# A two-layer encoder trunk on one core: moving the tiles in SBUF, weights to 0 and tokens to 64 modulo 128 bytes

## The chip, the cores and the metric

One core of a Trainium2 chip runs the whole program. The metric is the device time of one execution in microseconds; the kernel before takes 1598.72 us, the median of 3 runs (1597.99 to 1599.84).

## What is computed

Two encoder layers over 256 frames of width 1024, in float32. Layer 0 mixes with gated linear attention and retention and has a dense SwiGLU of width 3584; layer 1 mixes with a gated DeltaNet and has a mixture of 8 SwiGLU experts of width 3584, two for each frame.

```python
def swiglu(x, w_gu, w_down):
    gt, up = jnp.split(x @ w_gu, 2, axis=-1)
    return (jax.nn.silu(gt) * up) @ w_down

def reference(x, positions, ...):
    # layer 0
    h = mixer_gla_retention(x, positions, ab_w_in[0], ..., ab_w_out[0])
    x = layer_norm(DEEPNORM_ALPHA * x + h, ab_ln1_g[0], ab_ln1_b[0])
    x = layer_norm(DEEPNORM_ALPHA * x + swiglu(x, ffn_w_gu[0], ffn_w_down[0]), ...)
    # layer 1
    h = mixer_gated_deltanet(x, c_w_in[0], c_conv_w[0], ..., c_w_out[0])
    x = layer_norm(DEEPNORM_ALPHA * x + h, c_ln1_g[0], c_ln1_b[0])
    y = moe_swiglu(x, moe_w_router[0], moe_b_router[0], moe_w_gu[0], moe_w_down[0])
    return layer_norm(DEEPNORM_ALPHA * x + y, c_ln2_g[0], c_ln2_b[0])
```

## The kernel before

The work is a chain of large products with weights that are read once: mixer 0, the dense FFN, mixer 1, and the expert layer, which has most of the weights. To keep float32 accuracy every weight and every token value is split into a high and a low part of type `float32r`, and a product is three matmuls: high by high, low by high, high by low (`mm3`, `mm3w`).

Weights come in pieces of 1 MiB, one DMA each, into the tiles `wraw` (`load`). A piece is cut into two halves of 1024 columns for each partition (`cut`): ScalarE copies a half into `wh` (the high part), VectorE subtracts and writes `wl` (the low part). The halves go in turn through a ring of five buffers (`set_ring`): three lie in the pool `spl`, on the left of SBUF, two in the pool `keep`, on the right. In the expert layer the ring has only the three of `spl`, since `keep` is closed there (end of `mixer1`). A half is loaded again only when its matmuls are done.

Which operand moves through TensorE and which is stationary differs by stage:

- mixers 0 and 1, input and output projections (`proj`, `out_proj`): the weights move, up to 512 columns a matmul; the tokens are stationary (`xh`, `xl` in `keep`, in mixer 0's output projection `oh`, `ol`);
- dense FFN, gate and up (`ffn`, `gu`), and mixer 1's q, k and v: the tokens `xh`, `xl` move, 256 columns a matmul, and the weights are stationary; a half gives 24 matmuls;
- dense FFN, down: the weights move, 512 columns; the tokens `hh`, `hl` are stationary;
- expert layer (`gate_up_mm`, `down_mm`): the weights move, 512 columns; the tokens `xgh`, `xgl` and `hh`, `hl` (of the pool `mb`) are stationary.

The order of instructions on every engine is written out by the program itself (`manual_schedule`), with a planner (`Pace`) that counts on costs for each operation. Where a tile lies is not planned: pools are stacked one behind the other, from the left or from the right end, and a tile lies where the sum of the tiles before it puts it. In the operand names of the profile the moving operand stands first: `psA<-wh,xgh` moves `wh` past `xgh`.

Of the kernel before, what the change touches and what calls it, by code (L numbers as in the profile page):

```python
# [9 lines left out]
F32 = mybir.dt.float32  # L10
# [7 lines left out]
P = 128  # L18
# [97 lines left out]
FI = 6, 3, 3  # L116
GA = 1
FILL = 5, 1
class Pace:


# [2 lines left out]
    def __init__(self, nc):  # L124
        self.nc = nc
        self.clk = dict(tensor=0.0, vector=0.0, scalar=0.0, gpsimd=0.0, sync=0.0)
        self.spans, self.rings, self.base = {}, {}, {}
        self.cold, self.ops = 3000.0, 0
        for e in self.clk:
            setattr(self, e, Paced(self, e))  # L130
# [111 lines left out]
class Net:  # L242
    NSPL, NDENSE = 5, 2

    def __init__(self, ctx, tc, a, out):
        self.ctx, self.tc, self.nc, self.a, self.out = ctx, tc, Pace(tc.nc), a, out
        pool = lambda **k: ctx.enter_context(tc.tile_pool(**k))
        self.const = pool(name="const", bufs=1)
        self.slots = []
        self.raw_pool("raw", 3)  # L250
        self.spl = pool(name="spl", bufs=1)
        self.xe = pool(name="xe", bufs=2)
        self.ln = pool(name="ln", bufs=2)

        self.dense = ExitStack()
        self.keep = self.dense.enter_context(tc.tile_pool(name="keep", bufs=1, side="right"))
        self.ring = []
        self.psum = pool(name="psum", bufs=4, space=bass.MemoryType.PSUM)
        self.cst = {}
        self.tasks, self.live, self.tagB = [], 0, None  # L260
        self.pieces, self.halves, self.ready, self.loaded = [], [], {}, {}
        self.share, self.lows, self.pend = False, [], None
        self.n_dma = self.n_split = self.n_use = self.held = 0
# [180 lines left out]
        return t  # L444

    def bc(self):
        return self.keep.tile([P, D], F32, name="bc", tag="bc", bufs=2)

    def rstd(self, y, var, eps=EPS):
# [236 lines left out]
    def load_x(self):  # L686
        nc, a = self.nc, self.a
        self.load_const("cb", self.const, nc.sync)
        self.x = [self.new_x(0, b) for b in range(2)]
        for b in range(2):  # L690
            for c in range(2):
                cs = slice(c * 512, (c + 1) * 512)
                nc.sync.dma_start(self.x[b][:, cs], a["x"][b * P:(b + 1) * P, cs])
            if b == 0:
                self.load_next(1)
        self.xh = self.keep.tile([P, KT, T], F32R, name="xh", tag="xh")
        self.xl = self.keep.tile([P, KT, T], F32R, name="xl")
        self.load_next()

    def transpose_x(self, b, between=lambda: None):  # L700
# [6 lines left out]
    def mixer0(self):  # L707
# [4 lines left out]
        pool = es.enter_context(self.tc.tile_pool(name="m0", side="right", bufs=1))  # L712
        tmp = es.enter_context(self.tc.tile_pool(name="m0t", side="right", bufs=2))
        oh = pool.tile([P, KT, T], F32R, name="oh")
        ol = pool.tile([P, KT, T], F32R, name="ol")
        wg2 = pool.tile([17, 256], F32, name="wg2")
        nc.sync.dma_start(wg2[0:16], a["gla_w_gate2"])
        nc.sync.dma_start(wg2[16:17], a["gla_b_gate"].rearrange("(o n) -> o n", o=1))
# [276 lines left out]
        n_ = {k: c1 - c0 for k, (c0, c1) in self.AB.items()}  # L995
        self.fill(att[0][0][:, 0:P], FILL[0])
        self.held = 3
        engs = [nc.vector, nc.gpsimd]
        self.transpose_x(0, lambda: (self.fill(att[0][0][:, 0:P], FILL[1]), self.presplit(1, engs.pop(0))))
        pt = [self.ps("A") for _ in range(2)]  # L1000
# [640 lines left out]
    def moe_open(self):  # L1641

        nc, a, tc = self.nc, self.a, self.tc
        self.raw_pool("raw2", RO)
        self.load_next()
        self.mo = mo = self.ctx.enter_context(tc.tile_pool(name="mo", bufs=1))
        self.wr = mo.tile([P, KT, NE], F32, name="wr")
        nc.gpsimd.dma_start(self.wr, a["moe_w_router"].rearrange("(k p) e -> p k e", p=P))
        self.br = mo.tile([P, NE], F32, name="br")
        nc.gpsimd.dma_start(self.br, a["moe_b_router"].partition_broadcast(P))  # L1650
        self.load_const("c2", mo, nc.gpsimd)
        self.tri, self.one = self.c("tri0"), self.c("one").to_broadcast([P, P])
        self.xnh = [mo.tile([P, D], F32R, name="xnh", tag="xnh", bufs=2) for _ in range(2)]
        self.xnl = [mo.tile([P, D], F32R, name="xnl", tag="xnl", bufs=2) for _ in range(2)]
        self.lg = mo.tile([P, 2, NE], F32, name="lg")
        self.sel = mo.tile([P, 2, NE], F32, name="sel")
        self.comb = mo.tile([P, 2, NE], F32, name="comb")
        self.slot = mo.tile([P, 2, NE], F32, name="slot")
        self.t1 = mo.tile([P, 2], F32, name="t1")
        self.mx = mo.tile([P, 1], F32, name="mx")  # L1660
        self.cnt = mo.tile([P, 2, NE], F32, name="cnt")

    def natural_parts(self, b, x):

        self.nc.scalar.activation(self.xnh[b], x, AF.Copy)
        self.nc.gpsimd.tensor_tensor(self.xnl[b], x, self.xnh[b].bitcast(F32), OP.subtract)
# [390 lines left out]
    def moe_rest(self):  # L2057

        nc, a, tc = self.nc, self.a, self.tc
        slots, n = self.slots, [0]  # L2060

        def pieces(srcs):
            for src in srcs:
                wv = self.load(slots[n[0] % len(slots)], src)
                n[0] += 1
                for i in range(2):
                    yield self.cut(wv, i, 2)

        def run(gen):
            for _ in gen:  # L2070
                self.nc.clk["tensor"] += 50.0

        most = nc.values_load(self.most[0:1, 0:1], min_val=0, max_val=T)
        with tc.If(most > P):
            with tc.For_i(0, NE, 1) as e:
                pick = self.mb.tile([P, NE], F32, name="pick")
                nc.sync.dma_start(pick, a["eye"][bass.ds(e, 1)].rearrange("o n -> (o n)").partition_broadcast(P))
                t2 = self.mb.tile([P, 2, NE], F32, name="t2")
                sc = self.mb.tile([P, 2, 2], F32, name="sc")
                pb = pick[:, None, :].to_broadcast([P, 2, NE])  # L2080
                for i, src in enumerate((self.slot, self.comb)):
                    nc.vector.tensor_tensor(t2, src, pb, OP.mult)
                    nc.vector.tensor_reduce(sc[:, i], t2, axis=mybir.AxisListType.X, op=OP.add)
                nc.vector.tensor_scalar(sc[:, 0], sc[:, 0], -float(P), None, OP.add)
                s = self.new_s()[:, :, 0:P]
                self.onehot(s, 0, lambda b: sc[:, 0, b:b + 1])
                xg = self.new_xg()
                run(self.gather(s, [xg], [0]))
                acc = [self.ps("B") for _ in range(2)]
                wg = a["moe_w_gu"][bass.ds(e, 1)].rearrange("o k n -> (o k) n")  # L2090
                wd = a["moe_w_down"][bass.ds(e, 1)].rearrange("o k n -> (o k) n")
                for c in CUT:
                    pts = []
                    for u in range(2):
                        pt = [self.ps("A") for _ in range(c[1] // 512)]
                        for j, w in enumerate(pieces(self.gate_up(wg, c, u))):
                            self.gate_up_mm(pt, c, xg, j, w)
                            self.flush()
                        pts.append(pt)
                    hs = []  # L2100
                    run(self.hidden(self.silu(pts[0]), pts[1], hs))
                    for j, w in enumerate(pieces(self.down_rows(wd, c))):
                        self.down_mm(acc, c, hs, j, w)
                        self.flush()
                        self.hfree += j % 4 == 3
                st = []
                run(self.flip(s, st))
                run(self.scatter(st, acc, lambda b: sc[:, 1, b:b + 1]))
            for b in range(2):
                for c in range(2):  # L2110
                    self.ln_stats(self.y[b], self.st[:, b], c)
# [88 lines left out]
```

## Time and profile before

| | |
|---|---|
| time, median of 3 runs | 1598.72 us (1597.99 to 1599.84) |
| the profiled execution | 1597.8 us, of which the span from the first to the last instruction is 1596.0 |
| TensorE matmul | busy 1555.4 us, 97% of the span, 8467 instructions |
| TensorE weight load | 1332.8 us, 84% |
| VectorE | 1301.3 us, 82% |
| ScalarE | 1050.6 us, 66% |
| GpSimd | 160.5 us, 10% |
| DMA | 444.81 MB, mean 279 GB/s |
| mean granted TensorE clock | 0.992 |

Busy time is a share of the whole span, over stages with different limits, so the stages are read one by one. A busy TensorE says little by itself: the ends of matmuls are modelled and consecutive matmuls overlap in the trace, so what a matmul costs is read from the distance between two starts.

### The profile page before, as it was taken

What the parts mean: (1) busy time and instruction counts of PE and PEld (TensorE: products, weight loads), DVE (VectorE), ACT (ScalarE), POOL (GpSimd) and SP (SyncE); (2) the same over time, 40 slices, a digit from 0 to 9 for tenths busy, and PEclk for the clock granted to TensorE, in tenths of its full rate; (3) what the DMA queues carried; (4) which work ended last, traced back from release to release, by engine and by line L of the source; (5) the groups of instructions that cost most, each with busy time, mean ns of one, the idle gap of its engine ahead of it and who ended that gap; (6) DMA issues with size and microseconds to landing.
All of it is one profiled execution on the core that took longest, in us unless ns stands there. A gap on an engine that the chain in (4) does not pass through costs nothing.

```text
span 1596.0 us, 22720 instructions
## 1 busy us (share of the span) xinstructions
PE 1555.4 (97%) x8467; PEld 1332.8 (84%) x8467; DVE 1301.3 (82%) x1541; ACT 1050.6 (66%) x1239; POOL 160.5 (10%) x231
## 2 busy tenths in 40 slices
PE   9999999998999989999999999999999999999995
PEld 7788999997999968888888888888888888888884
DVE  5667555558867877999989999989999998999997
ACT  5345444445643347877877877878877778777774
POOL 5233000002361540000000000000000000000001
PEclk9999999999999989999999999999999999999998
DMA  7446555556313678999999999999999999999960
GB/s 265 134 159 223 190 198 192 185 168 198 97 47 106 226 275 294 376 370 350 372 347 341 367 368 362 367 362 335 369 368 363 360 375 328 369 366 368 361 219 28
DMA packets 161992, 444.81 MB, mean 279 GB/s; under 512 B 7553, under 2 KB 53778, under 8 KB 161874
## 3 DMA queue, kind: packets, MB, share of 16 engines
q1 hardware_dynamic: 160338, 437.98, 76.0%
q0 software_dynamic: 1536, 5.31, 1.1%
q8 instruction: 68, 1.11, 0.3%
q14 instruction: 50, 0.41, 0.1%
HBM read 442.21 MB, written 1.05 MB: 278 GB/s over the span
## 4 chain that ended last, share of the span: by engine, by line
PE 59%; issue 3%; DMA 0%; POOL 0%; DVE 0%; POOLq 0%; DVEq 0%
PE psA L223 37%; PE psB L223 21%; DMA gb<-in_c_ln_g_dram 0%; POOL x L223 0%; DVE wl L223 0%; POOLq L2196 0%; DVE xgl L223 0%; POOLq L223 0%; DVEq L223 0%
## 5 line engine op out<-in xcount | busy, mean ns | idle before, releaser
L223 DVE SCALAR_TENSOR_TENSOR wl<-wraw,wh 128x1024 fp32r<-128x1024 f32 (+2 forms) x824 | 992.7, 1223 | 199.0 <-ACT wh L223 147.1
L223 ACT ACTIVATE wh<-wraw 128x1024 fp32r<-128x1024 f32 (+3 forms) x835 | 863.1, 1052 | 265.2 <-PE psA L223 201.3
L223 PE MATMUL psA<-wh,xgh 128*128 128x512 f32 x894 | 291.0, 395 | 0.0
L223 PE MATMUL psA<-wh,xgl 128*128 128x512 f32 x894 | 288.3, 392 | 0.0
L223 PE MATMUL psA<-wl,xgh 128*128 128x512 f32 x894 | 279.4, 394 | 0.0
L223 PEld LDWEIGHTS psA<-wh,xgl 128*128 128x128 f32 x894 | 168.2, 188 | 37.2
L223 PEld LDWEIGHTS psA<-wh,xgh 128*128 128x128 f32 x894 | 166.9, 189 | 34.5
L223 PEld LDWEIGHTS psA<-wl,xgh 128*128 128x128 f32 x894 | 165.9, 188 | 34.8
L223 PE MATMUL psB<-wh,hh 128*128 128x512 f32 x560 | 183.3, 392 | 0.0
L223 PE MATMUL psB<-wh,hl 128*128 128x512 f32 x560 | 183.0, 392 | 0.0
L223 PE MATMUL psB<-wl,hh 128*128 128x512 f32 x560 | 182.8, 392 | 0.0
L223 PE MATMUL psA<-xh,wh 128*128 128x256 f32 x608 | 172.8, 284 | 0.0
L223 PE MATMUL psA<-xh,wl 128*128 128x256 f32 x608 | 170.0, 280 | 0.0
L223 PE MATMUL psA<-xl,wh 128*128 128x256 f32 x608 | 169.9, 280 | 0.0
L223 PEld LDWEIGHTS psB<-wh,hl 128*128 128x128 f32 x560 | 105.0, 188 | 23.5 <-DVE hl L223 0.9
L223 PEld LDWEIGHTS psB<-wl,hh 128*128 128x128 f32 x560 | 104.5, 188 | 22.3
L223 PEld LDWEIGHTS psB<-wh,hh 128*128 128x128 f32 x560 | 103.8, 188 | 20.6
L223 PEld LDWEIGHTS psA<-xh,wh 128*128 128x128 f32 x608 | 115.0, 189 | 1.4 <-issue 0.5
L223 PEld LDWEIGHTS psA<-xl,wh 128*128 128x128 f32 x608 | 115.0, 189 | 0.5
L223 PEld LDWEIGHTS psA<-xh,wl 128*128 128x128 f32 x608 | 115.0, 189 | 0.0
L223 POOL TENSOR_TENSOR x<-x,gb 128x256 f32<-128x256 f32 x4 | 4.2, 1069 | 993.8 <-ACT x L223 993.6
L223 PE MATMUL psA<-wh,xh 128*128 128x512 f32 (+4 forms) x224 | 74.1, 359 | 2.2 <-ACT wh L223 1.7
(298 smaller groups left out, 1449.5 us busy)
## 6 DMA issues: line engine op xcount, KB each, us to landing
wraw<-in_moe_w_gu_dram SPq DMA_DIRECT2D x224, 1024.0 KB, 6.2
wraw<-in_moe_w_down_dram SPq DMA_DIRECT2D x110, 1024.0 KB, 6.0
wraw<-in_ffn_w_gu_dram SPq DMA_DIRECT2D x26, 1024.0 KB, 5.1
wraw<-in_ffn_w_down_dram SPq DMA_DIRECT2D x14, 1024.0 KB, 4.9
wraw<-in_c_w_in_dram SPq DMA_DIRECT2D x12, 1024.0 KB, 5.7
wraw<-in_ab_w_in_dram SPq DMA_DIRECT2D x10, 1024.0 KB, 5.3
wraw<-in_ab_w_out_dram SPq DMA_DIRECT2D x4, 1024.0 KB, 4.9
wraw<-in_c_w_out_dram SPq DMA_DIRECT2D x4, 1024.0 KB, 7.0
```

What stands on the lines that cost most here:

```text
L223: r = f(*args, **kw)
```

## The change

Six tiles that nothing reads or writes are put into pools, and so the tiles that are allocated behind them move. No instruction is added or removed, and the rows of every engine's instruction stream, with their waits, are the same one by one.

```diff
+GAP = 16, 56, 8, 16
 ...
         self.const = pool(name="const", bufs=1)
+        self.const.tile([P, 24], F32, name="gap2")
 ...
-        self.ring = []
+        self.ring, self.gap = [], None
 ...
     def bc(self):
+        if not self.gap:
+            self.gap = self.keep.tile([P, GAP[1]], F32, name="gap1")
         return self.keep.tile([P, D], F32, name="bc", tag="bc", bufs=2)
 ...
         self.xl = self.keep.tile([P, KT, T], F32R, name="xl")
+
+        self.keep.tile([P, GAP[0]], F32, name="gap0")
 ...
         ol = pool.tile([P, KT, T], F32R, name="ol")
+        pool.tile([P, GAP[2]], F32, name="gap3")
 ...
         self.cnt = mo.tile([P, 2, NE], F32, name="cnt")
+        mo.tile([P, GAP[3]], F32, name="gap4")
 ...
                 sc = self.mb.tile([P, 2, 2], F32, name="sc")
+                self.mb.tile([P, 8], F32, name="gap5")
```

Where the operands of the large matmuls lie, as the allocator places them in the two programs (the first byte within a partition; buffers of one tile differ by multiples of 256):

| tiles | first buffer, before | modulo 256 | first buffer, after | modulo 256 |
|---|---|---|---|---|
| `wh`, `wl` in `spl` | 41632, 45728 | 160 | 41728, 45824 | 0 |
| `wh`, `wl` in `keep` | 204768, 208864 | 224 | 204544, 208640 | 0 |
| `xh`, `xl` (keep) | 188384, 196576 | 224 | 188096, 196288 | 192 |
| `oh`, `ol` (mixer 0) | 113344, 121536 | 192 | 113024, 121216 | 128 |
| `hh`, `hl` (dense FFN) | 160416, 166560 | 160 | 160128, 166272 | 128 |
| `xgh`, `xgl` (expert layer) | 199520, 207712 | 96 | 199488, 207680 | 64 |
| `hh`, `hl` (expert layer) | 215904, 220000 | 96 | 215872, 219968 | 64 |
| `wraw`, first three | 17056 | 160 | 17152 | 0 |

A matmul's operand is a slice of such a tile. Slices of these tiles begin at multiples of 512 bytes from its start (some of mixers 0 and 1, of 264, 336 and 352 columns, do not), so that a tile's place modulo 256 is that of all its matmul operands.

## Rows read from the trace of the kernel before

**Rows 1.** The stages of the span, one stretch a row: from:to in us, their length, then for each engine the us it was busy and its instructions, the granted TensorE clock, the mean busy share of the 16 DMA engines and what they moved. 0 to 200 is mostly mixer 0, 200 to 400 the dense FFN, 400 to 560 mixer 1, and from 640 on the expert layer.

```profile
0.00:200.00 200.00, 190.68 (x1192) 166.79 (x1193) 125.22 (x212) 93.45 (x119) 59.04 (x112) 0.99 0.59 195
200.00:400.00 200.00, 194.64 (x1385) 182.05 (x1384) 117.06 (x148) 92.44 (x116) 9.83 (x9) 1.00 0.57 187
400.00:560.00 160.00, 157.98 (x1284) 151.57 (x1283) 122.87 (x261) 70.90 (x123) 71.19 (x94) 1.00 0.37 122
640.00:900.00 260.00, 259.91 (x1182) 213.85 (x1181) 238.96 (x226) 205.82 (x227) 0.00 (x0) 1.00 0.98 361
900.00:1200.00 300.00, 299.90 (x1364) 246.37 (x1363) 276.57 (x262) 237.93 (x261) 0.00 (x0) 1.00 0.98 361
1200.00:1500.00 300.00, 300.00 (x1362) 246.85 (x1361) 277.62 (x264) 237.41 (x263) 0.00 (x0) 1.00 0.97 360
1500.00:1596.00 96.00, 79.83 (x357) 64.47 (x355) 81.05 (x81) 61.72 (x66) 4.24 (x4) 0.94 0.46 168
```

**Rows 2.** All instructions that write or read `wraw` from 640 to 1590 us: the two conversions with their least, median and greatest ns, then how long their engines sat idle before them and for whom, who waited for them, and the time from the issue of a load to its landing.

```profile
L223 DVE SCALAR_TENSOR_TENSOR wl<-wraw,wh x644: 1208/1225/1229, 638.9 to 1574.0; 128x1024 fp32r<-128x1024 f32 x161
L223 ACT ACTIVATE wh<-wraw x642: 1041/1061/1092, 639.6 to 1572.2; 128x1024 fp32r<-128x1024 f32 x161
...
  PE psA L223: 122.1, 393
  PE psB L223: 37.8, 139
...
who waited for it (us, times):
  DVE wl L223: 22.2, 36
  PEld psB L223: 1.0, 2
...
DMA to landing us min/median/max: 4.6/6.2/8.6
```

**Rows 3.** A stretch in which several loads were queued, columns as in rows 1.

```profile
570.00:580.00 10.00, 9.68 (x56) 8.07 (x54) 8.95 (x17) 3.45 (x6) 4.30 (x3) 1.00 1.02 408
```

**Rows 4.** TensorE's instructions in order of time in the expert layer, gate-up of one expert: start in us, length in us (from the start to the modelled end, so lengths overlap), what it is; a row marked x2 is two matmuls, the start is that of the first. From the first row to the last are 70 rows, 140 matmuls.

```profile
994.94 0.62 PE L223 MATMUL psA<-wh,xgh 128*128 128x512 f32 x2
995.40 0.62 PE L223 MATMUL psA<-wh,xgl 128*128 128x512 f32 x2
...
1026.99 0.62 PE L223 MATMUL psA<-wh,xgl 128*128 128x512 f32 x2
```

**Rows 5.** The same view in the dense FFN, gate-up on tiles of `spl`: 68 matmuls from the first row to the last.

```profile
208.43 0.28 PE L223 MATMUL psA<-xl,wh 128*128 128x256 f32 x1
208.54 0.28 PE L223 MATMUL psA<-xh,wl 128*128 128x256 f32 x1
...
216.14 0.28 PE L223 MATMUL psA<-xh,wh 128*128 128x256 f32 x1
```

**Rows 6.** The same view, gate-up on tiles of `keep`: 43 matmuls from the first row to the last.

```profile
258.73 0.28 PE L223 MATMUL psA<-xh,wl 128*128 128x256 f32 x1
258.85 0.28 PE L223 MATMUL psA<-xh,wh 128*128 128x256 f32 x1
...
263.88 0.28 PE L223 MATMUL psA<-xh,wh 128*128 128x256 f32 x1
```

**Rows 7.** The same view, gate-up on tiles of `spl` again, some 100 us later: 42 matmuls from the first row to the last.

```profile
308.36 0.28 PE L223 MATMUL psA<-xl,wh 128*128 128x256 f32 x1
...
313.31 0.28 PE L223 MATMUL psA<-xl,wh 128*128 128x256 f32 x1
```

**Rows 8.** The same view in mixer 0, an input projection on tiles of `spl`: 13 matmuls from the first row to the last.

```profile
18.46 0.40 PE L223 MATMUL psA<-wh,xl 128*128 128x512 f32 x1
18.70 0.39 PE L223 MATMUL psA<-wl,xh 128*128 128x512 f32 x1
...
21.50 0.39 PE L223 MATMUL psA<-wl,xh 128*128 128x512 f32 x1
```

**Rows 9.** The same view in mixer 0, an input projection on tiles of `keep`: 18 matmuls from the first row to the last.

```profile
28.08 0.39 PE L223 MATMUL psA<-wh,xh 128*128 128x512 f32 x1
...
32.16 0.39 PE L223 MATMUL psA<-wh,xh 128*128 128x512 f32 x1
```

**Rows 10.** The same view in the dense FFN, down projection on tiles of `keep`: 22 matmuls from the first row to the last.

```profile
202.82 0.39 PE L223 MATMUL psB<-wh,hh 128*128 128x512 f32 x1
203.05 0.39 PE L223 MATMUL psB<-wh,hl 128*128 128x512 f32 x1
...
207.85 0.39 PE L223 MATMUL psB<-wh,hl 128*128 128x512 f32 x1
```

**Rows 11.** Groups of TensorE's instructions over the whole span, by name and shape: out<-moving,stationary, stationary size, columns moved, count | us busy, mean ns of one | idle before. Each group has two sisters of the same count, with `xgl`, `hl`, `xl`, `ol` or `wl` in place of one operand.

```profile
L223 PE MATMUL psA<-wh,xgh 128*128 128x512 f32 x894 | 291.0, 395 | 0.0
L223 PE MATMUL psB<-wh,hh 128*128 128x512 f32 x560 | 183.3, 392 | 0.0
L223 PE MATMUL psA<-xh,wh 128*128 128x256 f32 x608 | 172.8, 284 | 0.0
L223 PE MATMUL psA<-wh,xh 128*128 128x512 f32 x112 | 45.1, 402 | 0.0
L223 PE MATMUL psA<-wh,oh 128*128 128x512 f32 x32 | 12.7, 398 | 0.0
```

## The prediction, made before the changed kernel ran

> **What bounds the kernel now.** I read the stages first, then the waits on the weight tiles, then the order of TensorE's matmuls in time. In the stages [rows 1] the expert layer shows as three long stretches from 640 to 1500 us in which TensorE is busy all the time at the full clock of 2.4 GHz, VectorE for 92% and ScalarE for 79%; in the dense FFN (200 to 400 us) TensorE is busy for 97%, and VectorE for 59%. DMA looks full too, at a share of 0.97 to 0.98 and some 361 GB/s, so the next view has to tell whether weights come late. They do not [rows 2]: the conversions wait for TensorE to release a buffer (122.1 us for `psA`, 37.8 for `psB`), nobody waits for a load, and TensorE's weight load waited for a conversion for 1.0 us in all. Where loads were queued, DMA moved 408 GB/s [rows 3], 13% more than the expert layer takes. So TensorE alone sets the time, and what counts is the distance from one matmul start to the next.
>
> In the expert layer that distance is (1026.99 - 994.94) / 140 = 228.9 ns [rows 4]. 512 columns at 2.4 GHz are 213.3 ns, so 15.6 ns of every matmul are something else.
>
> The same instruction has other distances on other buffers, and this is what the change touches. In the FFN's gate-up 256 token columns move past a weight slice. On weights in `spl` (160 modulo 256, tokens at 224) the distance is (216.14 - 208.43) / 68 = 113.4 ns [rows 5]; on weights in `keep`, at 224 as the tokens, it is 5.15 / 43 = 119.8 [rows 6]; on `spl` again, 100 us later and with the same offsets, 4.95 / 42 = 117.9 [rows 7]. So place matters, and what ran before matters as well. With 512 columns: mixer 0 on `spl` (weights 160, tokens 224) 3.04 / 13 = 233.8 [rows 8], on `keep` (both 224) 4.08 / 18 = 226.7 [rows 9], and the FFN's down projection on `keep` (weights 224, tokens 160) 5.03 / 22 = 228.6 [rows 10]. Let distance be the moving operand's first byte less the stationary one's, modulo 256. Then for 512 columns: 0 gives 226.7, +64 gives 228.6 and 228.9, -64 gives 233.8; for 256 columns: +64 gives 113.4 or 117.9, 0 gives 119.8. 113.4, 119.8, 226.7 and 233.8 are near 17, 18, 34 and 35 times 6.67 ns, the time of 16 columns, that is 64 bytes, at 2.4 GHz; the data alone would take 16 and 32 of these steps.
>
> **The change part by part.** It adds six tiles that nobody touches: no instruction, no wait, no DMA, the same order on every engine. All that is left is the place of operands. VectorE and ScalarE convert from and to tiles that move together (all from 160 to 0 for the first three); their 1225 and 1061 ns [rows 2] vary by 2% and 5% over all buffers that the expert layer uses, and they have 8% and 21% to spare [rows 1], so I cost them at nothing; if VectorE took 8% longer, it would be the bound. Loads have the 13% of above as cover.
>
> The expert layer. 3 x 894 gate-up and 3 x (560 - 112) down matmuls [rows 11], 4026 in all (112 of each `psB` group are the FFN's: 14 blocks, 2 halves, 2 token blocks, 2 column halves). Weights move from 160 to 0, tokens from 96 to 64: the distance turns from +64 to -64, and both operands now begin on a multiple of 64. No row shows such a pair, so it is bounded: below by one 64-byte step less than the lowest of the rows, 226.7 - 6.7 = 220.0, since a moving operand that begins at 32 modulo 64 touches 33 pieces of 64 bytes and an aligned one 32; above by 233.8, the row with -64. I take 226.7, between the ends and near to the +64 rows that it comes from: the half-piece at the start is gone for both operands, and the lowest spacing that rows reach is the cautious measure of that. 4026 x (228.9 - 226.7) = **-8.9 us**.
>
> FFN gate-up and mixer 1's q, k, v. 3 x 608 matmuls of 256 columns [rows 11]; a half gives 24, so 76 halves, and the ring gives 30 of them to `keep`: 720 matmuls at 119.8, the other 1104 at 113.4 or 117.9, on a mean of 115.6. Afterwards all are 64 apart (tokens 192, weights 0). With 115.6 for all: 720 x 4.2 = **-3.0 us**. Ends: all at 113.4, 720 x 6.4 + 1104 x 2.2 = -7.0 us; all at 119.8, 1104 x 4.2 = +4.6 us.
>
> Mixer projections of 512 columns. 3 x 112 matmuls [rows 11], some 204 on `spl` and 132 on `keep`. Weights 0, tokens 192: +64 for all, so 228.8: 204 x (233.8 - 228.8) = -1.0, 132 x (228.8 - 226.7) = +0.3: **-0.7 us**. Ends 220.0 and 233.8: -3.7 and +0.9 us.
>
> FFN down (336 matmuls, now 128 apart) and mixer 0's output projection (3 x 32 [rows 11], now 128 apart). No row has 128; between 226.7 and 233.8 the 432 matmuls can move by 432 x 7.1 = 3.1 us either way, and I take **0**.
>
> Sum: -8.9 - 3.0 - 0.7 = -12.6 us. On the profiled execution, 1597.8 us (span 1596.0 and 1.8 around it), that is 1585.2; against the median, 1598.72, it is **1586.1 us**. What is late next stays TensorE: VectorE's 92% of the expert layer becomes 93%.
>
> The Trainium skill, TensorE: Matmul & The Clock Gate, section "Part 2: What happens when you issue a matmul", says that TensorE has two independent read ports in SBUF, so that loading the next stationary operand takes no read bandwidth from the running matmul. By that rule places would not matter, and the sum would be 0 and the time 1598.7. The trace speaks against it, with 113.4 and 119.8 ns for one instruction on two buffers [rows 5, 6]. The same page, section "Back-to-back issue gap", gives N / 2.4 + 2.5 ns, 215.8 for 512 columns; a change that reached it would save 4026 x 13.1 = 53 us by this estimate, and no row here comes near.
>
> **The rivals.**
>
> *Slower: the sign of the distance decides.* With period 256, +64 and -64 are different places, and rows 8 and 10 say so: 233.8 against 228.6, both with three matmuls of different token parts in a row. The expert layer gets mixer 0's distance, -64, and would go to 233.8 in all 4026 matmuls, 4.9 ns each: +19.7 us. With -3.0 and -0.7 that is +16.0, 1614.7 us; if the 256-column matmuls, which also turn to -64, go to 119.8, +23.6, 1622.3 us. It decides as soon as the expert layer's distance rises by 3.7 us / 4026 = 0.9 ns. Against it: rows 8 and 9 begin at 32 modulo 64 with both operands, and afterwards none does.
>
> *No change: only the distance modulo 128 counts.* Then the expert layer stays at 228.9, as it is 64 apart before and after. The 720 matmuls gain 3.0 us, the 132 of the mixers on `keep` go to the 233.8 of their neighbours on `spl`, +0.9: -2.1 us, 1596.6 us. For it speaks that 64 apart is better than 0 with 256 columns; against it, that rows 8 and 10 differ. The change has an effect only through places, so this is also the case in which it does nothing. The Trainium skill's rule of two read ports (TensorE: Matmul & The Clock Gate, Part 2) ends in this case, at 1598.7 us.
>
> *Much faster: a whole step goes.* If the extra piece of 64 bytes is what each matmul pays, all 512-column matmuls lose 6.67 ns: (4026 + 336 + 432) x 6.67 = -32.0 us, and the 256-column ones go to 113.4, -7.0 us: 1559.7 us. TensorE's 228.9 ns would become 222.2, VectorE's share 95%, DMA's rate 372 GB/s, so nothing else would bind. For it: all distances lie on whole steps above the data. Against it: 226.7, which is 34 steps, is reached with the half-piece in place, so that piece need not be the extra one.
>
> **How the numbers follow.** Forecast 0.36, slower 0.32, no change 0.18, much faster 0.14. About 0.2% (3.2 us) is what a measurement of this kernel can tell from no change. Faster 0.36 + 0.14 = 0.50, same 0.18, slower 0.32. The range takes in the slower case up to where half of the 256-column loss comes with it, 1618 us, and the much faster one down to 1561; outside are about half of the much faster case and a quarter of the slower one. The likeliest case by itself spans 1577 to 1595 us, by a third of a step (2.2 ns) more or less for each matmul of the expert layer.
>
> **What would show it.** Right: in the expert layer 140 matmuls take 31.7 us instead of 32.05, and FFN gate-up shows no 119.8 any more, whatever the buffer. 32.7 us for 140 matmuls is the slower rival, 32.05 the third, 31.1 the fourth. In the stages TensorE stays at 100% and the stretches get shorter by the same share; conversions keep 1225 and 1061 ns. The forecast is wrong if the distance rises in the expert layer, if VectorE's conversions change, or if a load comes late there.

## The result: 0.8% slower, and the profile after

The changed kernel takes 1611.30 us, the median of 4 runs (1609.64 to 1612.09), against 1598.69 for the kernel before in the same comparison (4 runs, 1597.99 to 1599.84): a ratio of 1.008, 95% interval 1.0068 to 1.0093. The forecast was 1586.1. What came is close to the rival on the sign of the distance, 1614.7 us.

The stages after (columns as in rows 1), the dense FFN and one stretch of the expert layer:

```profile
200.00:400.00 200.00, 194.55 (x1405) 181.24 (x1404) 119.32 (x152) 93.80 (x118) 9.87 (x10) 1.00 0.57 186
900.00:1200.00 300.00, 299.88 (x1343) 242.27 (x1342) 273.06 (x259) 234.71 (x258) 0.00 (x0) 1.00 0.96 354
```

TensorE is busy all the time in the expert layer as before [rows 1], but it starts 1343 matmuls in 900 to 1200 us where it started 1364, and VectorE and ScalarE are less busy, not more (273.1 us against 276.6, and 234.7 against 237.9). DMA moves 354 GB/s instead of 361. There the other engines and the loads slowed with TensorE; the dense FFN got through more work (1405 matmuls in its 200 us, before 1385).

All instructions on `wraw` in the expert layer (the answer to rows 2):

```profile
L224 DVE SCALAR_TENSOR_TENSOR wl<-wraw,wh x642: 1210/1225/1229, 640.0 to 1587.9; 128x1024 fp32r<-128x1024 f32 x161
L224 ACT ACTIVATE wh<-wraw x641: 1043/1062/1092, 639.5 to 1586.0; 128x1024 fp32r<-128x1024 f32 x161
...
  PE psA L224: 151.9, 501
  PE psB L224: 54.0, 215
...
who waited for it (us, times):
  PEld psB L224: 1.1, 2
...
DMA to landing us min/median/max: 3.9/5.6/8.0
```

The conversions take 1225 and 1062 ns, as before. They wait longer for TensorE to release a buffer (151.9 and 54.0 us, before 122.1 and 37.8), and loads land after 5.6 us instead of 6.2. TensorE's weight load waited for a conversion for 1.1 us. So nothing feeds TensorE late: it needs longer for the same matmul.

The same stretch of TensorE's order in time as in rows 4, gate-up of one expert, 31 rows and so 62 matmuls from the first row to the last:

```profile
1017.49 0.63 PE L224 MATMUL psA<-wh,xgh 128*128 128x512 f32 x2
...
1031.96 0.63 PE L224 MATMUL psA<-wh,xgl 128*128 128x512 f32 x2
```

14.47 us / 62 = 233.4 ns, where it was 228.9 [rows 4] (the 140 there take in some down matmuls, which lie at the same distance). In the dense FFN, gate-up, 95 matmuls from the first row to the last:

```profile
257.54 0.28 PE L224 MATMUL psA<-xh,wh 128*128 128x256 f32 x1
...
268.31 0.28 PE L224 MATMUL psA<-xh,wl 128*128 128x256 f32 x1
```

10.77 / 95 = 113.4 ns, on buffers of `keep` and of `spl` alike: the 119.8 of `keep` [rows 6] and the 117.9 of [rows 7] are gone from this stage. Mixer 0's input projections, 17 matmuls on one kind of buffer and 22 on the other:

```profile
18.60 0.39 PE L224 MATMUL psA<-wh,xh 128*128 128x512 f32 x1
...
22.49 0.39 PE L224 MATMUL psA<-wl,xh 128*128 128x512 f32 x1
...
28.55 0.39 PE L224 MATMUL psA<-wh,xl 128*128 128x512 f32 x1
...
33.60 0.39 PE L224 MATMUL psA<-wl,xh 128*128 128x512 f32 x1
```

3.89 / 17 = 228.8 and 5.05 / 22 = 229.5 ns, where they were 233.8 [rows 8] and 226.7 [rows 9]. And the FFN's down projection, 23 matmuls:

```profile
202.56 0.39 PE L224 MATMUL psB<-wh,hh 128*128 128x512 f32 x1
...
207.91 0.40 PE L224 MATMUL psB<-wl,hh 128*128 128x512 f32 x1
```

5.35 / 23 = 232.6 ns, before 228.6 [rows 10].

### The profile page after: what moved, and what is told of

Read it like the earlier page. It is cut to its first block, busy times and chain, and to the rows that moved or that the text cites. A ratio compares the mean times of both kernels' runs of the same rounds, so it can differ in the third digit from the quotient of the medians.

```text
span 1609.8 us, 22720 instructions
## 1 busy us (share of the span) xinstructions
PE 1570.5 (98%) x8467; PEld 1331.2 (83%) x8467; DVE 1303.8 (81%) x1541; ACT 1051.7 (65%) x1239; POOL 161.4 (10%) x231
## 4 chain that ended last, share of the span: by engine, by line
PE 59%; issue 3%; DMA 0%; POOL 0%; DVE 0%; POOLq 0%; DVEq 0%
PE psA L224 38%; PE psB L224 22%; DMA gb<-in_c_ln_g_dram 0%; POOL x L224 0%; DVE wl L224 0%; POOLq L2205 0%; POOLq L224 0%; DVEq L224 0%
## 5 line engine op out<-in xcount | busy, mean ns | idle before, releaser
L224 PE MATMUL psA<-wh,xgl 128*128 128x512 f32 x894 | 291.8, 396 | 0.0
L224 PE MATMUL psA<-wl,xgh 128*128 128x512 f32 x894 | 283.2, 398 | 0.0
L224 PEld LDWEIGHTS psA<-xh,wl 128*128 128x128 f32 x608 | 114.2, 188 | 0.0
L224 PE MATMUL psA<-wh,xl 128*128 128x512 f32 (+4 forms) x224 | 72.9, 355 | 4.2 <-DVE xl L224 4.2
```

What stands on the lines that cost most here:

```text
L224: r = f(*args, **kw)
```

## The experiments

The theories. **A**: the spacing is set by the signed distance, the moving operand's first byte less the stationary one's, modulo 256; it does not matter where both begin. **B**: it is the start on a multiple of 64 bytes that costs, for both operands. **C**: places modulo 128 alone count, or the loads and conversions that collide with TensorE's reads, and the expert layer's loss is by another way than its matmuls' distance.

### Matmuls alone, by distance

```diff
+BLOCKS = [...]  # 48 matmuls of 512 columns for each distance 0, 32, ... 480
+                # then four odd distances, four with both operands 32 further,
+                # and 96 matmuls of 256 columns for each distance 0, 32, ... 224
+nc.tensor.matmul(p[:, 0:n], st[name][:, q:q + 128], wf[:, o:o + n], ...)
```

> The matmuls by themselves: blocks of 48 float32r matmuls of 512 columns (96 of 256 columns), back to back, each block with another place of its operands; nothing else runs, and the output is only x. It computes nothing of the reference. Blocks sa to sp: 512 columns, distance (moving less stationary first byte) 0, 32, ... 480, both from multiples of 32. ta to td: distances 16, 48, 80, 208. ua to ud: distances 0, 64, 128, 192 with both operands 32 bytes further. va to vh: 256 columns, distances 0, 32, ... 224. Theory A (only the signed distance modulo 256 counts): si to sp repeat sa to sh; 0 gives 226.7 ns from start to start, 64 gives 228.9, 128 gives 232.5, 192 gives 233.3; ua to ud repeat these four; 256 columns: 0 gives 120, 192 gives 113.4, 64 gives 113.4 or 117.8. Theory B (an operand that begins on a multiple of 64 is what makes the expert layer slow): ua and ub are some 4 ns below sa and sc, whatever the distance. Theory C (the matmuls don't depend on places by themselves, it takes the traffic of the other engines): all blocks of 512 columns are equal.

TensorE's order in time, one block a row (start, length, what; `sa` is distance 0, `sb` 32, and so on to `sj`, 288; `ua` to `ud` are 0, 64, 128 and 192 with both operands 32 bytes further; `va`, `vb`, `vc` are 0, 32 and 64 with 256 columns). The spacing of a block is the difference of two starts, divided by its count:

```profile
20.91 11.05 PE L45 MATMUL acc<-w,sa 128*128 128x512 f32 x48
31.80 11.35 PE L45 MATMUL acc<-w,sb 128*128 128x512 f32 x48
42.99 11.16 PE L45 MATMUL acc<-w,sc 128*128 128x512 f32 x48
53.99 11.36 PE L45 MATMUL acc<-w,sd 128*128 128x512 f32 x48
65.19 11.36 PE L45 MATMUL acc<-w,se 128*128 128x512 f32 x48
76.38 11.40 PE L45 MATMUL acc<-w,sf 128*128 128x512 f32 x48
87.62 11.36 PE L45 MATMUL acc<-w,sg 128*128 128x512 f32 x48
98.82 11.36 PE L45 MATMUL acc<-w,sh 128*128 128x512 f32 x48
110.03 11.05 PE L45 MATMUL acc<-w,si 128*128 128x512 f32 x48
120.92 11.35 PE L45 MATMUL acc<-w,sj 128*128 128x512 f32 x48
...
243.47 11.07 PE L45 MATMUL acc<-w,ua 128*128 128x512 f32 x48
254.38 11.16 PE L45 MATMUL acc<-w,ub 128*128 128x512 f32 x48
265.37 11.32 PE L45 MATMUL acc<-w,uc 128*128 128x512 f32 x48
276.52 11.36 PE L45 MATMUL acc<-w,ud 128*128 128x512 f32 x48
287.72 11.66 PE L45 MATMUL acc<-w,va 128*128 128x256 f32 x96
299.22 11.37 PE L45 MATMUL acc<-w,vb 128*128 128x256 f32 x96
310.42 11.47 PE L45 MATMUL acc<-w,vc 128*128 128x256 f32 x96
```

| distance modulo 256 | 0 | 32 | 64 | 96 | 128 | 160 | 192 | 224 |
|---|---|---|---|---|---|---|---|---|
| 512 columns, ns | 226.9 | 233.1 | 229.2 | 233.3 | 233.1 | 234.2 | 233.3 | 233.5 |
| both operands 32 further | 227.3 | | 229.0 | | 232.3 | | 233.3 | |
| 256 columns, ns | 119.8 | 116.7 | 117.9 | 119.9 | 118.6 | 117.3 | 117.8 | 118.3 |

At 256 the row begins anew (`si`, 226.9). +64 and -64 (192) differ by 4.1 ns with 512 columns, and moving both operands to 32 modulo 64 changes less than 1 ns. ScalarE still writes operands of later blocks until 38.6 us, in the middle of `sb`; from there on nothing runs but matmuls and their weight loads, and `si` and `sj` repeat `sa` and `sb`. That is A with no other engine and no load at work; B and C fall. Of the multiples of 32 only 0 and, less so, 64 are better than the rest with 512 columns. The four odd distances, 16, 48, 80 and 208, give 228.5, 231.7, 230.0 and 233.3 ns, so the spacing does not move in steps of 64 bytes. With 256 columns the order is another one, and 0 is among the worst.

### The expert layer alone, back at +64, and at 0

The two edits differ in one number. The first undoes the part of the change that concerns the expert layer's distance, while all operands keep their new multiples of 64; the second tries the best distance of 512 columns.

```diff
-                self.mb.tile([P, 8], F32, name="gap5")
+                self.mb.tile([P, 40], F32, name="gap5")   # distance +64
```

> The changed kernel with the tokens of the expert layer 128 bytes lower: distance +64 there, as in the kernel before, weights still at 0 modulo 256, tokens at 192. Theory A (signed distance modulo 256): 4026 matmuls go from 233.3 back to 228.9 ns, 17.7 us less than the changed kernel, 1593.6 us. Theory B (multiples of 64 hurt): both operands still begin on one, so it stays at 1611. Theory C (the loss lies in conversions or loads, whose tiles are not moved here): stays at 1611.

```diff
-                self.mb.tile([P, 8], F32, name="gap5")
+                self.mb.tile([P, 24], F32, name="gap5")   # distance 0
```

> The changed kernel with the tokens of the expert layer 64 bytes lower: distance 0 there, weights and tokens both at 0 modulo 256. Theory A: 226.7 ns, 4026 x 6.6 = 26.6 us less than the changed kernel, 1584.7 us, and 14 us faster than the kernel before. A theory that wants 64 between weights and tokens (modulo 128): no better than the changed kernel, 1611 or above. Theory B: stays at 1611.

The first takes 1593.29 us (1592.26 to 1595.51, 7 runs), the second 1584.92 (1583.17 to 1585.34, 5 runs); the kernel before 1598.24 (12 runs) beside them. The ratios to before are 0.9969 (0.9957 to 0.9982) and 0.9910 (0.9894 to 0.9925). Gate-up of one expert in the first, 62 matmuls from row to row:

```profile
1009.88 0.62 PE L224 MATMUL psA<-wh,xgh 128*128 128x512 f32 x2
...
1024.07 0.62 PE L224 MATMUL psA<-wh,xgl 128*128 128x512 f32 x2
```

and in the second, also 62:

```profile
1005.19 0.62 PE L224 MATMUL psA<-wh,xgh 128*128 128x512 f32 x2
...
1019.24 0.62 PE L224 MATMUL psA<-wh,xgl 128*128 128x512 f32 x2
```

14.19 / 62 = 228.9 and 14.05 / 62 = 226.6 ns. Both operands begin on multiples of 64 here as in the changed kernel, so B has nothing left. Sizes agree too: 4026 x (233.4 - 228.9) = 18.1 us, measured 1611.30 - 1593.29 = 18.0; 4026 x (233.4 - 226.6) = 27.4, measured 26.4.

### The kernel before, with its expert layer at -64

```diff
                 sc = self.mb.tile([P, 2, 2], F32, name="sc")
+                self.mb.tile([P, 32], F32, name="gap5")
```

> The kernel before with one part of the change alone, its sign in the expert layer: tokens there 128 bytes lower, so weights at 160, tokens at 224, distance -64 instead of +64; both still at 32 modulo 64, and 64 apart modulo 128 as before. Theory A: 233.3 instead of 228.9 ns in 4026 matmuls, +17.7 us, 1616.4 us. Theory B and a period of 128: no change, 1598.7 us.

1615.44 us (1615.19 to 1617.13, 4 runs), ratio 1.0105 (1.0088 to 1.0123). Gate-up, 54 matmuls:

```profile
1022.67 0.63 PE L223 MATMUL psA<-wh,xgh 128*128 128x512 f32 x2
...
1035.27 0.63 PE L223 MATMUL psA<-wh,xgh 128*128 128x512 f32 x2
```

12.60 / 54 = 233.3 ns. Weights begin at 160 and tokens at 224 modulo 256 here, each at 32 modulo 64, and the spacing is that of the changed kernel with its multiples of 64. The sign of the distance is enough to make the kernel before slower, with every tile of the dense stages where it was: 4026 x (233.3 - 228.9) = 17.7 us, measured 1615.44 - 1598.24 = 17.2.

### 256 columns: what ran before

In the kernel the gate-up matmuls went at 113.4, alone at 117.8 for the same distances. The second kernel of matmuls keeps the kernel's order (`xh` past `wh`, `xl` past `wh`, `xh` past `wl`), and puts blocks of 512 columns ahead.

```diff
+for name, d in ONE:            # each distance: 96 matmuls of 256 columns
+    narrow(name, d, 32)
+for n, _, p, q in TWO:         # 24 of 512 columns at p, then 48 of 256 at q
+    wide("p" + n, p, 24)
+    narrow("q" + n, q, 16)
```

> A kernel of matmuls alone, no product of the reference: first 96 matmuls of 256 columns for each distance 0, 32, ... 224, in the order high-high, high-low, low-high as in the dense FFN; then eight pairs of a block of 24 matmuls of 512 columns at distance 0, 64, 128 or 192 and a block of 48 matmuls of 256 columns at 64 or at 192. If distance alone sets the spacing, the blocks at 64 and at 192 show one number each wherever they stand, near the 117.8 ns of the first sweep. If what ran just before decides (the FFN showed 113.3 and 117.8 ns at the same distance), the same block shows 113.4 behind some of the 512-column blocks and 117.8 behind others. If the order high-high, high-low, low-high decides, all blocks at 64 and 192 show 113.4.

Blocks `qa` and `qc`, both at distance 64, `qa` behind a block of 512 columns at distance 0 (`pa`), `qc` behind one at 128 (`pc`); 46 matmuls from the first to the last row of each:

```profile
115.87 5.61 PE L41 MATMUL acc<-xh,pa 128*128 128x512 f32 x24
121.32 0.28 PE L41 MATMUL acc<-xh,qa 128*128 128x256 f32 x1
...
126.74 0.28 PE L41 MATMUL acc<-xl,qa 128*128 128x256 f32 x1
...
138.12 5.75 PE L41 MATMUL acc<-xh,pc 128*128 128x512 f32 x24
143.71 0.28 PE L41 MATMUL acc<-xh,qc 128*128 128x256 f32 x1
...
148.92 0.28 PE L41 MATMUL acc<-xl,qc 128*128 128x256 f32 x1
```

(126.74 - 121.32) / 46 = 117.8 and (148.92 - 143.71) / 46 = 113.3 ns, for the same instruction on the same distance. All eight:

| 512 columns ahead at | 0 | 64 | 128 | 192 |
|---|---|---|---|---|
| then 256 columns at 64 | 117.8 | 117.8 | 113.3 | 117.8 |
| then 256 columns at 192 | 117.8 | 117.8 | 113.4 | 113.4 |

So 256 columns at 64 or 192 have two steady spacings; in these eight pairs, each run once, it goes with the block ahead which of them holds, and it then holds for the whole block. The order of the three matmuls does not decide it (the blocks of 96 in this order gave 117.8 at both distances). Distance alone, as theory A had it, is not enough for 256 columns.

### The down and output projections at distance 0 too

This asks whether the gain of the second expert edit can be had in the dense stages too, or whether the 256-column matmuls take it back. The expert layer stays at 0; only the mixers' input projections keep +64.

```diff
-GAP = 16, 56, 8, 16
+GAP = 16, 56, 40, 16                                       # oh, ol: distance 0
...
             self.split(hh, hl, t)
             hs[0] = hh, hl
+            pool.tile([P, 32], F32, name="gap6", bufs=1)   # hh, hl: distance 0
```

> The version with distance 0 in the expert layer (1584.9 us), with the FFN's hidden parts and mixer 0's output operands moved as well, so that all 512-column matmuls but the mixers' input projections are at distance 0. Distance alone: 336 down matmuls go from 232.5 to 227 or 228.3, 96 output projection matmuls from 232.5 to 227: -1.9 and -0.5 us, 1582.5 us, gate-up stays at 113.4. If what ran before decides the spacing of the 256-column matmuls: gate-up behind a down projection at distance 0 went at 117.8 in the kernel before, and up to 1344 gate-up matmuls of the FFN rise from 113.4 to 117.8, +5.9 us: up to 1588.4 us.

1589.18 us (1587.77 to 1591.13, 5 runs; before 1598.19, 9 runs), ratio 0.9944 (0.9931 to 0.9958): 4.3 us above the version it builds on, which ran on another chip, and their two ratios to the kernel before are clear of each other. Its down projection (23 matmuls) and its gate-up (95):

```profile
204.03 0.39 PE L224 MATMUL psB<-wh,hh 128*128 128x512 f32 x1
...
209.25 0.39 PE L224 MATMUL psB<-wl,hh 128*128 128x512 f32 x1
...
259.71 0.28 PE L224 MATMUL psA<-xh,wh 128*128 128x256 f32 x1
...
270.90 0.28 PE L224 MATMUL psA<-xh,wl 128*128 128x256 f32 x1
```

The same in the version with the expert layer alone at 0:

```profile
203.31 0.39 PE L224 MATMUL psB<-wh,hh 128*128 128x512 f32 x1
...
208.65 0.40 PE L224 MATMUL psB<-wl,hh 128*128 128x512 f32 x1
...
258.28 0.28 PE L224 MATMUL psA<-xh,wh 128*128 128x256 f32 x1
...
269.06 0.28 PE L224 MATMUL psA<-xh,wl 128*128 128x256 f32 x1
```

Down got what distance promises, 5.22 / 23 = 227.0 instead of 5.34 / 23 = 232.2 ns, and gate-up went from 10.78 / 95 = 113.5 to 11.19 / 95 = 117.8, in all twelve blocks of 96 that stand behind a down projection; the one block of 96 ahead of them, behind other work, went at 113.7 from neighbour to neighbour (114.8 in the version it builds on). (These are 1152 matmuls and not the 1344 of the expectation: of the FFN's 14 blocks the first moves weights.) 1152 x 4.4 - 336 x 5.2 = +3.3 us; in the two traces the time from the first of these blocks to the first of mixer 1's q, k, v blocks is 219.8 and 216.5 us, +3.3. Mixer 0's output projection gained its 96 x 6.3 ns = 0.6 us. A better distance for one matmul brought the worse spacing for the next.

With the down projection at +64 instead:

```diff
+            pool.tile([P, 48], F32, name="gap6", bufs=1)   # hh, hl: distance +64
```

> The same version with distance 0 in the expert layer (1584.9 us), with only the FFN's hidden parts moved, so that the down projection is at distance +64. Distance alone: 336 matmuls from 232.5 to 229.3, -1.1 us, 1583.8 us, gate-up stays at 113.4. If what ran before decides the spacing of the 256-column matmuls, gate-up can change to 117.8 in a part of the FFN: up to +5.9 us, 1589.7 us.

1586.61 us (1583.89 to 1586.92, 5 runs), ratio 0.9922 (0.9909 to 0.9936). Its down projection (23 matmuls) and its gate-up (95):

```profile
201.70 0.39 PE L224 MATMUL psB<-wh,hh 128*128 128x512 f32 x1
...
206.96 0.39 PE L224 MATMUL psB<-wl,hh 128*128 128x512 f32 x1
...
256.39 0.28 PE L224 MATMUL psA<-xh,wh 128*128 128x256 f32 x1
...
267.18 0.28 PE L224 MATMUL psA<-xh,wl 128*128 128x256 f32 x1
```

Down went at 5.26 / 23 = 228.7 and gate-up at 10.79 / 95 = 113.6 ns, and the FFN stretch took 215.7 us, 0.8 less than 216.5, near the 1.1 of distance alone. The total does not show it: 1586.6 and 1584.9 are from two chips, and the intervals overlap. Gate-up at 113.6 behind a block at +64 is also not what the table of eight pairs says (117.8); so the block ahead is not named well enough by its distance. Nor does the order of work settle it alone: up to the expert layer the changed kernel and its version with the expert layer at +64 are the same program on the same places, and yet mixer 1's first 84 matmuls of 256 columns, which come behind a wait, went at 113.3 ns in the one trace and 117.8 in the other, and the next 108 at 117.8 and 113.3.

## Why the prediction was wrong

- **What bounds the kernel**: right. TensorE's spacing sets the time, and no other engine, wait or load shows in what changed.
- **The expert layer, -8.9 us**: this step failed. It took 226.7 ns, on the ground that the half-piece at the start is gone for both operands; measured 233.4, that is 4026 x (233.4 - 228.9) = +18.1 us. The bounds, 220.0 and 233.8, held it, and the range of the time held 1611.3 only because it took in the slower rival. No run shows the half-piece, nor a step of 64 bytes: with both operands at 32 modulo 64 the sweep gives 227.3 at distance 0 against 226.9 on multiples of 64, and 233.3 at -64 either way. The row with -64 [rows 8] was the nearest in the one quantity that the prediction had itself defined, and it was taken for the far bound because the expert layer was thought of as starting near the +64 rows.
- **256 columns, -3.0 us**: the sign was right, the size too small. FFN gate-up went to 113.4 everywhere, mixer 1 kept some of its 117.8. Over all undisturbed stretches of the two traces the mean spacing was 119.8 on `keep` and 115.3 on `spl`, and is now close to 114.2 on both: 720 x 5.6 + 1104 x 1.1 = -5.2 us. The dense part as a whole is read from the edit that takes the expert layer back to +64: 1593.29 - 1598.24 = -5.0 us, where the terms said -3.7. Why 113.4 is open: gate-up stands behind a down projection that is now 128 apart, and behind 128 both distances fall into 113.4 in the pairs, but behind a down projection at +64 it went at 113.6 too. The forecast left out another product of mixer 1, the 128 matmuls of `S` past `xnh` and `xnl`, which `gap4` moves from distance 128 to 192: undisturbed they went from 120 to 114 ns, at most -0.8 us.
- **Mixers, -0.7 us**: right, 228.8 and 229.5 for both kinds of buffer.
- **Down and output projection, 0 within 3.1 us**: 128 costs more than thought: 232.6 instead of 228.6 ns, 336 x 4.0 = +1.3 us, inside the bounds. Rows 10 show `keep` alone; over all 336, on both pools, the two traces have 228.8 and 232.3, +1.2 us. The output projection's 96 went at 233.2 before and after. (The tokens of these two go to 128 modulo 256, not to the 64 modulo 128 of the title.)
- **The sum** with these values: +18.1 - 5.0 = +13.1, measured 1611.30 - 1598.69 = +12.6 us.
- **The rivals**: "the sign of the distance decides" came true, with 233.4 for 233.8 in the expert layer and the dense gain larger than its -3.7. What spoke against it (rows 8 and 9 begin at 32 modulo 64) was no evidence. "No change" fell with the expert layer's 233.4, "much faster" with the sweep, where no distance comes below 226.9 ns; in the expert layer at 0 it was 226.6.
- **What would show it**: 140 expert matmuls at 233.4 are 32.7 us, the number named for this rival; no 119.8 in gate-up and unchanged conversions came as forecast.

The Trainium skill states that the stationary operand is loaded through a read port of its own and that this takes no read bandwidth from the running matmul (TensorE: Matmul & The Clock Gate, Part 2: What happens when you issue a matmul). By itself that does not explain these runs: with nothing but matmuls and their weight loads running, the same instruction is spaced 226.9 to 234.2 ns by the distance between its two operands. Why the spacing depends on that distance is not settled by these runs, nor what chooses between 113.4 and 117.8.

## What to carry to other kernels

When matmuls are back to back on an engine that sets the time, tabulate their spacing by the signed distance of the two operands before moving tiles, and take the row with the same distance rather than an argument on alignment. For `float32r` with 512 columns distance 0 modulo 256 was best here; one dead tile of 96 bytes a partition in place of 32 in the expert pool turned a kernel 0.8% slower than before into one 0.9% faster. After such a move look at the stages that were not to change: moving the down projection's tokens altered the spacing of the gate-up behind it.

## What the runs showed of the hardware

- The spacing of back-to-back `float32r` matmuls depends on the first byte of the moving operand less that of the stationary one, modulo 256: 226.9 ns at 0, 228.5 at 16, 229.2 at 64, 233.1 to 234.2 at the other multiples of 32 (512 columns, full clock, matmuls alone); 228.9, 226.6 and 233.4 at 64, 0 and 192 in the expert layer.
- +64 and -64 are different (229.2 and 233.3), and moving both operands by 32 bytes changes it by less than 1 ns.
- With 256 columns the order is different: 119.8 at 0, and at 64 and 192 two steady spacings, 113.4 and 117.8. The distance of the block ahead can change which one holds (the FFN's gate-up went at 113.5 behind a down projection at 128 and at 117.8 behind one at 0), but it does not name it in every case.
- Conversions on VectorE and ScalarE did not react when all the tiles that they read and write moved together modulo 256: 1225 and 1061 ns at 160, 1225 and 1062 at 0.
